# A new instruction order for a group of a two-level Strassen-like matmul, fills in one operation, W as one tile

## The chip, the cores and the metric

The kernel runs on one core of one Trainium2 chip. The metric is the time of one execution in microseconds (us), as the device measures it; lower is better. One run of it was also taken by the hardware profiler, and all lines shown here come from that profiled execution.

## The reference

The reference makes a running sum of `x` along the rows and takes neighbouring differences of it, which gives `x` back but for rounding, and multiplies by `w`:

```python
B, S, D = 8, 2048, 2048
cs = np.cumsum(x, axis=1)
diff = cs - np.concatenate([zeros((B, 1, D)), cs[:, :-1, :]], axis=1)
return np.matmul(diff, w).astype(np.float32)
```

So what has to be computed is `x @ w` with `x` of 16384 x 2048 and `w` of 2048 x 2048, float32 in and out.

## The kernel before

The 16384 rows are 128 row tiles of 128 rows (`t`). The first four are multiplied plainly in bf16 while `w` comes in from HBM; the next four (`group_plain`) and the four after those (`group_half`) go over to the scheme of the main part. The main part is 29 groups of four row tiles each (`class Group`), and these make most of the time.

**Arithmetic of a group.** The four tiles of a group are called g, h, k, l. Two pairs of tiles and the halves of `w` form one level of a seven-product scheme (Winograd's form of Strassen's), and five of its seven products (`P1` to `P5`) are split once more in the same way, into seven quarters `p1` to `p7`. A quarter is four matmuls of 128x512 (`quarter`, line 561); `P6` and `P7` aren't split and are made in eight steps of four matmuls each (`steps`, line 542). That makes 5 x 7 + 2 x 8 = 51 PE steps and 204 matmuls a group. In the step names `P3.p2` is quarter p2 of product P3, and `P6h.1` a step of P6 for tiles of h.

**Around the matmuls.** Every row tile comes as two halves of 512 KB: `load0`, `load1` (line 100, SP queue, into the five slots of the tile `F`), `weigh0`, `weigh1` (ACT, line 112: sum of absolute values), `scale` (two small DVE instructions, lines 128 and 130), `unit` (POOL, line 136), `narrow0`, `narrow1` (ACT, line 147: to fp16, in place), and `turn0`, `turn1` (line 160: DMA transposes on the SP queue into the x tiles). DVE then makes the sums of halves: `S1` to `S4` over whole tiles and `P1.s1` and the like over quarters (line 532). Results come out of PSUM banks by `keep` (ACT, line 569: scale into a buffer `c`), `add` (DVE, line 572: scale and add into the same buffer) and `put` (line 583: 256 KB to HBM on the SP queue). There are seven such buffers in a first-in, first-out list `free`: a `keep` takes the head, a `put` gives its buffer back at the tail. Copies and merges between banks are `P1.cg`, `P1.ct`, `P2.cv` (ACT, line 1014) and `P1.m1`, `P1.m2` (DVE, line 1021). Banks go the same way through the list `open_banks`.

**The passing buffer.** Weights of the second level that have no place of their own pass through one tile `flow` of four blocks of 512: by DVE (`P1.fp4`, `P3.fp2`, `P5.fp4`, `P5.fp5`, line 928, four subtractions or additions of 512 columns each), or from HBM (`P2.fp4`, `P4.fp4`, line 525, 512 KB). A fill has to wait until the quarter that used the buffer before has been read out.

**What sets the order.** It is written out by hand in the string `ORDER`: names of steps with the group that they belong to, as an offset (`load0.g+1` is the load of the next group). Each round of the loop walks the string once, and `after` chains each instruction to the one before it on its engine, so every engine, and the SP queue, runs its instructions in exactly this order. `END_ORDER` is the order of the last steps of the last group. Two pieces of preparation stand in the first group only: `before` puts two subtractions ahead of `P1.s4` and four (`in_5.third`) ahead of `P5.s3`.

Of the kernel before, what the change touches and what calls it, by code (L numbers as in the profile page):

```python
# [10 lines left out]
def kernel(  # L11
# [6 lines left out]
    nc = tc.nc  # L18
    P = 128
# [28 lines left out]


    const = ctx.enter_context(tc.tile_pool(name="const", bufs=1))  # L50
    W = [const.tile([P, 4 * NH], f32, name=f"W{k}") for k in range(KH)]
    whole = [t.rearrange("p (a h n) -> p a h n", a=2, h=2) for t in W]
    pieces = [
        t.bitcast(f16).rearrange("p (i n j c) -> p i j n c", i=4, j=2, c=NB) for t in W
    ]
    B11, T1, B12, T2, B21, T3, B22, T4 = (
        [p[:, i // 2, i % 2] for p in pieces] for i in range(8)
    )
    uw = const.tile([P, 1], f32, name="uw")
    uinv = const.tile([P, 1], f32, name="uinv")  # L60

# [29 lines left out]
    unit = {}  # L91
# [4 lines left out]
    def load(t, i):  # L96
        if t < END:
            after(
                "sp",
                lambda: nc.sync.dma_start(  # L100
                    where[t][i], x2[ds(t * P, P), ds(i * NH, NH)]
                ),
            )
# [51 lines left out]
    def turn(t, halves=range(2)):  # L155
        if t < END:
            for i in halves:
                after(
                    "sp",
                    lambda: nc.sync.dma_start_transpose(  # L160
                        place(t)[i], narrowed(t)[:, ds(i * NH, NH)]
                    ),
                )

    def alone(shape, dtype, name, until=ctx):
        pool = until.enter_context(tc.tile_pool(name=f"{name}_", bufs=1))
        return pool.tile(shape, dtype, name=name)

    with ExitStack() as head:
# [138 lines left out]
        for ko in range(KO - KQ):  # L308
# [9 lines left out]
            if ko in turns:  # L318
                q, a = turns[ko]
# [149 lines left out]
    spills = ctx.enter_context(  # L469
        tc.tile_pool(name="spills", bufs=1, space=bass.MemoryType.DRAM)  # L470
    )
    S1 = [alone([P, 2, NB], f16, f"S1{i}") for i in range(2)]
    inner = alone([P, 20, NB], f16, "inner")
    flow = alone([P, 4, NB], f16, "flow")
    spill = [spills.tile([P, 4, NB], f16, name=f"spill{i}") for i in range(1, 3)]
# [43 lines left out]
    passed = [flow[:, k, :] for k in range(4)]  # L519
# [15 lines left out]
    def steps(to, a, b, first, pieces):  # L535
        for i in range(pieces):
            ks = range(i * KH // pieces, (i + 1) * KH // pieces)

            def some():
                for k in ks:  # L540
                    for n in range(2):
                        said = nc.tensor.matmul(  # L542
                            to[n],
                            a[k],
                            b[k][:, n, :],
                            start=(first and k == 0),
                            stop=(k == KH - 1),
                            skip_group_check=True,
                        )
# [42 lines left out]
    def parts(t):  # L592
        return [Part(a.rearrange("p (n k) m -> p n (k m)", n=2)) for a in place(t)]
# [16 lines left out]
    in_2, in_3 = Inner(B21), Inner(B22)  # L610
    in_3.Q4 = [spare.pop() for _ in range(4)]
    in_4, in_5 = Inner(T4), Inner(T1)
    for i in (in_2, in_4, in_5):
        i.Q4 = passed
    assert not spare
    in_1 = Inner(B11, (in_5.Q1, [t.all[:, n, :] for t in reversed(S1) for n in range(2)]))

    def group_plain(g, X, Y, Z, V):
        h = g + 2
# [122 lines left out]
    def group_half(g, X, Y, q, e, v, w):  # L742
# [179 lines left out]
        put(C21h[0], h + 1, 0)  # L922
        turn(next_l, [1])

    def fill_by(op, a, b):
        def some():
            for k in range(4):
                after("dve", lambda: nc.vector.tensor_tensor(passed[k], a[k], b[k], op))  # L928

        return some  # L930

    sevens = {
        "P1": (in_1, {"p4": fill_by(SUB, in_1.t21, in_1.Q2)}),
        "P2": (in_2, {"p4": lambda: bring_flow(1)}),
        "P3": (in_3, {"p2": fill_by(ADD, in_3.Q4, in_3.Q2)}),
        "P4": (in_4, {"p4": lambda: bring_flow(2)}),
        "P5": (
            in_5,
            {
                "p4": fill_by(SUB, in_5.t21, in_5.Q2),  # L940
                "p5": fill_by(SUB, in_5.t22, in_5.Q2),
            },
        ),
    }
# [3 lines left out]
    class Group:  # L948
# [112 lines left out]
        def plan(self):  # L1061
# [46 lines left out]
            for a, b in ("gk", "hl"):  # L1108
                (A11, A12), (A21, A22) = half[a], half[b]
                self.step(f"S1.{a}", total, A21, A21, A22, ADD)  # L1110
                self.step(f"S2.{a}", total, A11, A21, A11, SUB)
# [73 lines left out]
                    self.step(f"{P}{c}.{j}", some, a, to, j)  # L1185

    ORDER = """
    P2.s3+0 keep.C11g0+0 P1.p2+0 load0.g+1 P1.s3+0 keep.C21h0-1 P1.p3+0 P1.p7+0
    P2.cv+0 S1.g+0 S2.g+0 P2.s4+0 P2.p6+0 P1.m2+0 keep.C11h1+0 add.C21h0.x-1
    load1.g+1 P1.fp4+0 turn0.l+0 P2.p2+0 P5.p1+0 add.C11h1.e+0 add.C11g0.v+0  # L1190
    keep.C11g1+0 P6g.0+0 turn1.l+0 add.C11g1.q+0 S1.h+0 P5.s1+0 put.C12g1-1
    put.C21h0-1 weigh0.g+1 P1.p4+0 S2.h+0 P2.p3+0 add.C11g1.e+0 P5.cg+0 P2.fp4+0
    S4.g+0 P2.p7+0 P5.s2+0 weigh1.g+1 load0.h+1 P5.p2+0 scale.g+1 unit.g+1
    put.C11g0+0 keep.C11h0+0 add.C11h1.q+0 load1.h+1 P6g.2+0 weigh0.h+1 P6h.1+0
    P6g.1+0 P5.s4+0 P2.p4+0 P5.s3+0 P6g.3+0 keep.C22g0+0 P6h.0+0 P5.fp5+0 S4.h+0
    P3.s1+0 narrow0.g+1 P5.p5+0 P5.ct+0 put.C21h1-1 put.C11h1+0 keep.C12g0+0
    load0.k+1 weigh1.h+1 keep.C12g1+0 P4.s1+0 put.C11g1+0 P3.fp2+0 P5.p6+0
    narrow1.g+1 S3.g+0 add.C11h0.q+0 put.C11h0+0 P6h.2+0 put.C21g1-1 scale.h+1
    P6h.3+0 keep.C12h1+0 P3.s2+0 P3.s4+0 P3.p2+0 P3.p1+0 load1.k+1 P7g.1+0
    add.C12g0.q+0 P7g.2+0 keep.C12h0+0 P3.p6+0 narrow0.h+1 P7g.3+0 add.C12g0.z+0  # L1200
    P7g.0+0 S3.h+0 P7h.2+0 P3.s3+0 turn1.g+1 add.C12g1.q+0 P3.p7+0 P5.m1+0
    P5.p7+0 unit.h+1 turn0.g+1 P5.fp4+0 weigh0.k+1 narrow1.h+1 add.C22g0.x+0
    put.C22g0+0 P7h.1+0 weigh1.k+1 P7h.0+0 load1.l+1 unit.l+0 add.C12h1.q+0
    scale.k+1 put.C12g0+0 unit.k+1 narrow0.k+1 narrow1.k+1 P5.p3+0 keep.C22g1+0
    P5.m2+0 keep.C22h1+0 add.C12h0.q+0 load0.l+1 P5.p4+0 add.C12h1.z+0 P4.s3+0
    P4.fp4+0 P7h.3+0 P4.s2+0 P4.s4+0 add.C22h1.x+0 add.C22g1.x+0 put.C22g1+0
    P4.p1+0 P4.p2+0 turn0.h+1 keep.C22h0+0 keep.C21g0+0 P3.p5+0 add.C12g1.e+0
    P3.p3+0 add.C22h0.x+0 turn1.k+1 put.C22h0+0 put.C22h1+0 add.C21g0.x+0
    add.C12h1.e+0 P4.p6+0 P3.p4+0 turn1.h+1 add.C12g1.z+0 add.C12h0.z+0
    put.C12h1+0 P1.s1+1 P4.p5+0 keep.C21g1+0 weigh0.l+1 P1.p1+1 P1.cg+1  # L1210
    put.C21g0+0 P4.p3+0 P4.p4+0 keep.C21h1+0 add.C21g1.x+0 turn0.k+1
    add.C21g1.q+0 put.C12h0+0 P2.p1+1 P4.p7+0 P1.s2+1 P1.p5+1 P1.s4+1 weigh1.l+1
    P1.p6+1 add.C21h1.e+0 P2.s1+1 P1.ct+1 scale.l+1 add.C21h1.q+0 P1.m1+1
    narrow0.l+1 narrow1.l+1 P2.s2+1 P2.p5+1
    """
    ORDER = [(s[:-2], int(s[-2:])) for s in ORDER.split()]
    early = max(n for _, n in ORDER)
# [15 lines left out]
        for s in ("load0", "load1", "weigh0", "weigh1", "scale", "unit", "narrow0", "narrow1", "turn0", "turn1"):  # L1233
            del groups[0].do[f"{s}.{c}"]
    del groups[1].do["load0.g"], groups[1].do["load1.g"]
    before = {"P1.s4": lambda: less(in_1.Q2[2:], in_1.t22[2:], in_1.Q1[2:]), "P5.s3": in_5.third}
    for b in range(-early, len(groups) - late):
        for name, ahead in ORDER:
            i = b + ahead
# [39 lines left out]
```

## Time and profile before

| | |
|---|---|
| median of 3 runs | 1502.03 us (1501.6 to 1503.25) |
| the profiled execution, its own time | 1505.42 us |
| its span, first to last instruction | 1503.6 us |
| mean granted clock of TensorE | 0.996 |
| busy: PE / DVE / ACT / POOL | 1456.9 / 1284.5 / 973.5 / 60.5 us |
| HBM read / written | 181.40 / 135.27 MB |

Busy PE is overlapped time: a 128x512 matmul is shown with about 379 ns from start to end, while the next one starts well before that end. So a short hold of PE does not show as idle time in full. A row of a timeline holds equal instructions that follow each other, with the start, the time from the first start to the last end, their number, and in brackets the idle time before them and what ended it.

### The profile page before, as it was taken

How to read it: one execution, taken by the hardware profiler on the slowest of the kernel's cores; microseconds unless marked ns; L12 is line 12 of the kernel's file. 1: busy time of each engine (PE TensorE's matmuls, PEld its weight loads, DVE VectorE, ACT ScalarE, POOL GpSimd, SP SyncE). 2: the span in 40 equal slices, each digit the busy share in tenths (PEclk: the TensorE clock that was granted, in tenths of full speed). 3: DMA queues.
4: the chain of work that ended last, by engine and by line, in shares of the span. 5: the costliest groups of instructions: out<-in, count | busy, mean ns of one | idle time of the engine just before them, and what ended most of it. 6: DMA issues, size and time to landing. Idle time of an engine off the chain costs nothing.

```text
span 1503.6 us, 20817 instructions
## 1 busy us (share of the span) xinstructions
PE 1456.9 (97%) x6679; PEld 652.7 (43%) x6679; DVE 1284.5 (85%) x2645; ACT 973.5 (65%) x1446; POOL 60.5 (4%) x136
## 2 busy tenths in 40 slices
PE   8999999999999999999999999999999999999998
PEld 3444444444444444444444444444444444444443
DVE  7999988887888888888888788888889888888887
ACT  5887466665666766666657566666676566676662
POOL 0110000000000000000000000000000000000000
PEclk9999999999999999999999999999999999999999
DMA  9999888899899999889999889998899988899984
GB/s 364 360 245 276 235 242 258 258 246 263 217 257 259 253 269 242 234 262 256 252 252 236 245 261 246 273 243 257 249 264 251 275 236 255 252 253 263 259 225 147
DMA packets 386397, 383.09 MB, mean 255 GB/s; under 512 B 275760, under 2 KB 275760, under 8 KB 386160
## 3 DMA queue, kind: packets, MB, share of 16 engines
q1 hardware_dynamic: 385728, 379.93, 90.2%
q0 software_dynamic: 560, 1.84, 0.3%
q8 instruction: 52, 0.85, 0.2%
q14 instruction: 57, 0.47, 0.1%
HBM read 181.40 MB, written 135.27 MB: 211 GB/s over the span
## 4 chain that ended last, share of the span: by engine, by line
PE 67%; DMA 17%; DVE 11%; ACT 3%; issue 2%; SPq 1%; DVEq 0%; ACTq 0%
PE b L561 38%; PE b L542 26%; DMA x<-F 10%; DVE c L572 4%; DMA out_dram<-c 4%; DVE x L532 3%; PE b L264 2%; DVE inner L532 2%; DMA W<-in_w_dram 2%; DMA F<-in_x_dram 1%; ACT c L569 1%; DVE b L1021 1%; ACT F L147 1%; SPq L160 1%; DMA W<-in_x_dram 0%
## 5 line engine op out<-in xcount | busy, mean ns | idle before, releaser
L572 DVE SCALAR_TENSOR_TENSOR c<-b,of,c 128x512 f32<-128x512 f32 x790 | 564.2, 744 | 114.7 <-ACT c L569 70.6
L542 PE MATMUL b<-W,x 128*128 128x512 f16 x2144 | 509.3, 381 | 20.0 <-ACT c L569 15.5
L569 ACT ACTIVATE c<-b,of 128x512 f32<-128x512 f32 x492 | 321.7, 683 | 276.2 <-PE b L561 137.3
L561 PE MATMUL b<-W,x 128*128 128x512 f16 x1892 | 453.0, 379 | 10.9 <-DVE c L572 10.8
L561 PEld LDWEIGHTS <-x 128*128 128x128 f16 x2488 | 243.4, 98 | 318.7 <-issue 33.6
L112 ACT ACTIVATE waste<-F 128x1024 uint8<-128x1024 f32 x246 | 259.0, 1053 | 113.6 <-DMA F<-in_x_dram 113.0
L542 PEld LDWEIGHTS <-x 128*128 128x128 f16 x2144 | 210.4, 98 | 278.9 <-issue 16.2
L147 ACT ACTIVATE F<-F,of 128x1024 f16<-128x1024 f32 x246 | 282.0, 1146 | 53.8 <-DVE of L130 51.5
L532 DVE TENSOR_TENSOR x<-x,x 128x1024 f16<-128x1024 f16 (+1 forms) x388 | 221.4, 583 | 43.9 <-DMA x<-F 37.4
L561 PEld LDWEIGHTS <-inner 128*128 128x128 f16 x1648 | 161.2, 98 | 195.3 <-DVE inner L532 1.7
L561 PE MATMUL b<-W,inner 128*128 128x512 f16 x944 | 232.8, 379 | 0.5 <-DVE inner L532 0.5
L561 PE MATMUL b<-flow,x 128*128 128x512 f16 x588 | 151.7, 380 | 4.1 <-DVE c L572 4.0
L561 PE MATMUL b<-inner 128*128 128x512 f16 x472 | 121.1, 379 | 0.0
L136 POOL TENSOR_SCALAR of<-of,uw 128x1 f32<-128x1 f32 x124 | 55.6, 459 | 1337.2 <-DVE of L128 1329.2
L928 DVE TENSOR_TENSOR flow<-W 128x512 f16<-128x512 f16 x232 | 82.8, 418 | 6.0 <-PE b L561 5.8
L1021 DVE TENSOR_TENSOR b<-b,c 128x512 f32<-128x512 f32 x116 | 80.0, 690 | 2.5 <-PE b L561 2.4
L1014 ACT COPY b<-b 128x512 f32<-128x512 f32 x87 | 50.1, 575 | 24.4 <-PE b L561 13.1
L264 PE MATMUL b<-wb,xP 128*128 128x512 bf16 x240 | 57.4, 393 | 4.5 <-ACT wb L248 3.1
L1014 ACT COPY c<-b 128x512 f32<-128x512 f32 x58 | 33.6, 580 | 37.5 <-PE b L561 37.4
L532 DVE TENSOR_TENSOR inner<-x 128x512 f16<-128x512 f16 x117 | 49.3, 422 | 7.6 <-DMA x<-F 5.2
L532 DVE TENSOR_TENSOR inner<-x,inner 128x512 f16<-128x512 f16 x117 | 49.2, 421 | 4.0
L532 DVE TENSOR_TENSOR inner<-inner,x 128x512 f16<-128x512 f16 x117 | 48.4, 413 | 0.1
(69 smaller groups left out, 528.7 us busy)
## 6 DMA issues: line engine op xcount, KB each, us to landing
F<-in_x_dram SPq DMA_DIRECT2D x246, 512.0 KB, 5.9
out_dram<-c SPq DMA_DIRECT2D x492, 256.0 KB, 3.4
flow<-spill SPq DMA_DIRECT2D x58, 512.0 KB, 4.4
W<-in_w_dram SPq DMA_DIRECT2D x32, 512.0 KB, 9.5
W<-in_x_dram SPq DMA_DIRECT2D x16, 256.0 KB, 7.5
x<-F SPq DMA_TRANSPOSE x246, 3.5
out_dram<-o POOLq DMA_DIRECT2D x5, 256.0 KB, 4.0
out_dram<-o SPq DMA_DIRECT2D x5, 256.0 KB, 3.5
```

The costliest lines, as they stand in the source:

```text
L112: lambda: nc.scalar.activation(waste, where[t][i], ABS, scale=1.0 / ROW, accum_out=sums_of[t][:, i : i + 1],),
L136: after("pool", lambda: nc.gpsimd.tensor_scalar(u, m, uw, None, MUL))
L147: lambda: nc.scalar.activation(narrowed(t)[:, ds(i * NH, NH)], where[t][i], COPY, scale=s),
L264: lambda: nc.tensor.matmul(ps[r][n], xP[:, r, ko, :], wb[h, ko][:, ds(n * NB, NB)], start=(ko == 0), stop=(ko == KO - 1),),
L532: after("dve", lambda: nc.vector.tensor_tensor(dst.all, p.all, q.all, op))
L542: said = nc.tensor.matmul(to[n], a[k], b[k][:, n, :], start=(first and k == 0), stop=(k == KH - 1), skip_group_check=True,)
L561: said = nc.tensor.matmul(to, a[k], b[k], start=(first and k == 0), stop=(k == 3), skip_group_check=True)
L569: after("act", lambda: nc.scalar.activation(c, p, COPY, scale=u))
L572: after("dve", lambda: nc.vector.scalar_tensor_tensor(c, p, u, c, MUL, ADD))
L928: after("dve", lambda: nc.vector.tensor_tensor(passed[k], a[k], b[k], op))
L1014: after("act", lambda: nc.scalar.copy(c, p))
L1021: after("dve", lambda: nc.vector.tensor_tensor(t, p, s, ADD))
```

## The change

There are three parts to it. `W` becomes one tile instead of eight, and `S1` one tile instead of two, so that a view can reach over four blocks (`quarter_of`, `spare_of`). `fill_by` then makes one DVE instruction of 2048 columns instead of four of 512. For this the blocks of `in_1.Q2` lie in `S1` in the opposite order, and the two halves of its preparation change places (one in `group_half`, one in `before`). And the string `ORDER` is another permutation of the same steps; in it some steps belong to another round than before (for example `load0.g+2` in place of `load0.g+1`). `END_ORDER` stays.

```diff
--- before.py
+++ after.py
@@ -48,7 +48,8 @@
 
 
     const = ctx.enter_context(tc.tile_pool(name="const", bufs=1))
-    W = [const.tile([P, 4 * NH], f32, name=f"W{k}") for k in range(KH)]
+    W_all = const.tile([P, KH, 4 * NH], f32, name="W")
+    W = [W_all[:, k, :] for k in range(KH)]
     whole = [t.rearrange("p (a h n) -> p a h n", a=2, h=2) for t in W]
     pieces = [
         t.bitcast(f16).rearrange("p (i n j c) -> p i j n c", i=4, j=2, c=NB) for t in W
@@ -56,6 +57,16 @@
     B11, T1, B12, T2, B21, T3, B22, T4 = (
         [p[:, i // 2, i % 2] for p in pieces] for i in range(8)
     )
+    blocks = W_all.bitcast(f16).rearrange(
+        "p k (i n j c) -> p i j k n c", i=4, j=2, c=NB
+    )
+
+    def quarter_of(i, a, n):
+        return blocks[:, i // 2, i % 2, ds(4 * a, 4), n, :]
+
+    def spare_of(i, k):
+        return blocks[:, i // 2, i % 2, ds(k, 2), :, :]
+
     uw = const.tile([P, 1], f32, name="uw")
     uinv = const.tile([P, 1], f32, name="uinv")
 
@@ -469,7 +480,8 @@
     spills = ctx.enter_context(
         tc.tile_pool(name="spills", bufs=1, space=bass.MemoryType.DRAM)
     )
-    S1 = [alone([P, 2, NB], f16, f"S1{i}") for i in range(2)]
+    S1_all = alone([P, 4, NB], f16, "S1")
+    S1 = [S1_all[:, ds(2 * i, 2), :] for i in range(2)]
     inner = alone([P, 20, NB], f16, "inner")
     flow = alone([P, 4, NB], f16, "flow")
     spill = [spills.tile([P, 4, NB], f16, name=f"spill{i}") for i in range(1, 3)]
@@ -613,7 +625,7 @@
     for i in (in_2, in_4, in_5):
         i.Q4 = passed
     assert not spare
-    in_1 = Inner(B11, (in_5.Q1, [t.all[:, n, :] for t in reversed(S1) for n in range(2)]))
+    in_1 = Inner(B11, (in_5.Q1, [S1_all[:, i, :] for i in range(4)]))
 
     def group_plain(g, X, Y, Z, V):
         h = g + 2
@@ -887,7 +899,7 @@
         unit_of(next_l)
         in_4.third()
         load(then, 1)
-        less(in_1.Q2[:2], in_1.t22[:2], in_1.Q1[:2])
+        less(in_1.Q2[2:], in_1.t22[2:], in_1.Q1[2:])
 
         a11, a12, a22, s1, s2, s3, s4 = A4
         Q = in_4
@@ -922,23 +934,26 @@
         put(C21h[0], h + 1, 0)
         turn(next_l, [1])
 
+    def in_twos(t):
+        return t if len(t.shape) == 4 else t.rearrange("p (a b) n -> p a b n", a=2)
+
     def fill_by(op, a, b):
         def some():
-            for k in range(4):
-                after("dve", lambda: nc.vector.tensor_tensor(passed[k], a[k], b[k], op))
+            x, y = (in_twos(t) for t in (a, b))
+            after("dve", lambda: nc.vector.tensor_tensor(in_twos(flow), x, y, op))
 
         return some
 
     sevens = {
-        "P1": (in_1, {"p4": fill_by(SUB, in_1.t21, in_1.Q2)}),
+        "P1": (in_1, {"p4": fill_by(SUB, quarter_of(0, 1, 0), S1_all)}),
         "P2": (in_2, {"p4": lambda: bring_flow(1)}),
-        "P3": (in_3, {"p2": fill_by(ADD, in_3.Q4, in_3.Q2)}),
+        "P3": (in_3, {"p2": fill_by(ADD, spare_of(2, 0), inner[:, 16:20, :])}),
         "P4": (in_4, {"p4": lambda: bring_flow(2)}),
         "P5": (
             in_5,
             {
-                "p4": fill_by(SUB, in_5.t21, in_5.Q2),
-                "p5": fill_by(SUB, in_5.t22, in_5.Q2),
+                "p4": fill_by(SUB, quarter_of(1, 1, 0), quarter_of(6, 1, 0)),
+                "p5": fill_by(SUB, quarter_of(1, 1, 1), quarter_of(6, 1, 0)),
             },
         ),
     }
@@ -1185,33 +1200,33 @@
                     self.step(f"{P}{c}.{j}", some, a, to, j)
 
     ORDER = """
-    P2.s3+0 keep.C11g0+0 P1.p2+0 load0.g+1 P1.s3+0 keep.C21h0-1 P1.p3+0 P1.p7+0
-    P2.cv+0 S1.g+0 S2.g+0 P2.s4+0 P2.p6+0 P1.m2+0 keep.C11h1+0 add.C21h0.x-1
-    load1.g+1 P1.fp4+0 turn0.l+0 P2.p2+0 P5.p1+0 add.C11h1.e+0 add.C11g0.v+0
-    keep.C11g1+0 P6g.0+0 turn1.l+0 add.C11g1.q+0 S1.h+0 P5.s1+0 put.C12g1-1
-    put.C21h0-1 weigh0.g+1 P1.p4+0 S2.h+0 P2.p3+0 add.C11g1.e+0 P5.cg+0 P2.fp4+0
-    S4.g+0 P2.p7+0 P5.s2+0 weigh1.g+1 load0.h+1 P5.p2+0 scale.g+1 unit.g+1
-    put.C11g0+0 keep.C11h0+0 add.C11h1.q+0 load1.h+1 P6g.2+0 weigh0.h+1 P6h.1+0
-    P6g.1+0 P5.s4+0 P2.p4+0 P5.s3+0 P6g.3+0 keep.C22g0+0 P6h.0+0 P5.fp5+0 S4.h+0
-    P3.s1+0 narrow0.g+1 P5.p5+0 P5.ct+0 put.C21h1-1 put.C11h1+0 keep.C12g0+0
-    load0.k+1 weigh1.h+1 keep.C12g1+0 P4.s1+0 put.C11g1+0 P3.fp2+0 P5.p6+0
-    narrow1.g+1 S3.g+0 add.C11h0.q+0 put.C11h0+0 P6h.2+0 put.C21g1-1 scale.h+1
-    P6h.3+0 keep.C12h1+0 P3.s2+0 P3.s4+0 P3.p2+0 P3.p1+0 load1.k+1 P7g.1+0
-    add.C12g0.q+0 P7g.2+0 keep.C12h0+0 P3.p6+0 narrow0.h+1 P7g.3+0 add.C12g0.z+0
-    P7g.0+0 S3.h+0 P7h.2+0 P3.s3+0 turn1.g+1 add.C12g1.q+0 P3.p7+0 P5.m1+0
-    P5.p7+0 unit.h+1 turn0.g+1 P5.fp4+0 weigh0.k+1 narrow1.h+1 add.C22g0.x+0
-    put.C22g0+0 P7h.1+0 weigh1.k+1 P7h.0+0 load1.l+1 unit.l+0 add.C12h1.q+0
-    scale.k+1 put.C12g0+0 unit.k+1 narrow0.k+1 narrow1.k+1 P5.p3+0 keep.C22g1+0
-    P5.m2+0 keep.C22h1+0 add.C12h0.q+0 load0.l+1 P5.p4+0 add.C12h1.z+0 P4.s3+0
-    P4.fp4+0 P7h.3+0 P4.s2+0 P4.s4+0 add.C22h1.x+0 add.C22g1.x+0 put.C22g1+0
-    P4.p1+0 P4.p2+0 turn0.h+1 keep.C22h0+0 keep.C21g0+0 P3.p5+0 add.C12g1.e+0
-    P3.p3+0 add.C22h0.x+0 turn1.k+1 put.C22h0+0 put.C22h1+0 add.C21g0.x+0
-    add.C12h1.e+0 P4.p6+0 P3.p4+0 turn1.h+1 add.C12g1.z+0 add.C12h0.z+0
-    put.C12h1+0 P1.s1+1 P4.p5+0 keep.C21g1+0 weigh0.l+1 P1.p1+1 P1.cg+1
-    put.C21g0+0 P4.p3+0 P4.p4+0 keep.C21h1+0 add.C21g1.x+0 turn0.k+1
-    add.C21g1.q+0 put.C12h0+0 P2.p1+1 P4.p7+0 P1.s2+1 P1.p5+1 P1.s4+1 weigh1.l+1
-    P1.p6+1 add.C21h1.e+0 P2.s1+1 P1.ct+1 scale.l+1 add.C21h1.q+0 P1.m1+1
-    narrow0.l+1 narrow1.l+1 P2.s2+1 P2.p5+1
+    keep.C11g1+0 add.C11h1.e+0 P2.p2+0 add.C11g1.q+0 add.C21g1.x-1 P2.p3+0
+    turn1.l+0 add.C11g1.e+0 P6g.3+0 P2.s3+0 P5.p1+0 P5.cg+0 P2.fp4+0 P6g.1+0
+    weigh0.g+1 S1.h+0 P5.s1+0 keep.C11h0+0 P5.s2+0 P2.p7+0 add.C11h1.q+0
+    put.C21g0-1 load1.g+1 S2.h+0 P6g.0+0 put.C21h1-1 P6g.2+0 add.C11g0.v+0
+    keep.C12g1+0 P5.s4+0 P2.p4+0 put.C11h1+0 add.C11h0.q+0 P5.p6+0 P5.fp5+0
+    P6h.1+0 put.C21g1-1 load0.h+1 S4.g+0 weigh1.g+1 P6h.0+0 keep.C12g0+0
+    put.C11h0+0 P5.p2+0 keep.C22g0+0 put.C11g1+0 S3.g+0 P5.p5+0 S4.h+0 P6h.2+0
+    P5.ct+0 P3.s1+0 P7g.2+0 P5.m1+0 scale.g+1 narrow0.g+1 P6h.3+0 P5.s3+0
+    P4.s1+0 P5.p7+0 put.C11g0+0 P7g.0+0 P5.fp4+0 P5.m2+0 load1.h+1 P7g.3+0
+    P4.s2+0 S3.h+0 narrow1.g+1 P5.p4+0 load0.k+1 load1.k+1 keep.C12h0+0 P7g.1+0
+    keep.C12h1+0 P3.fp2+0 P3.s2+0 turn0.g+1 P5.p3+0 weigh0.h+1 add.C22g0.x+0
+    put.C22g0+0 P3.s4+0 P4.s4+0 P3.p2+0 weigh1.h+1 P7h.0+0 keep.C22g1+0
+    add.C12g0.z+0 keep.C22h0+0 add.C22g1.x+0 scale.h+1 P4.fp4+0 P3.s3+0 P7h.2+0
+    put.C22g1+0 P3.p1+0 add.C12g0.q+0 turn1.g+1 narrow0.h+1 keep.C22h1+0
+    add.C12h1.z+0 P7h.1+0 P7h.3+0 add.C22h0.x+0 add.C22h1.x+0 put.C22h0+0
+    P3.p6+0 add.C12g1.q+0 P3.p3+0 weigh0.k+1 P3.p5+0 P3.p4+0 add.C12g1.z+0
+    P4.s3+0 weigh1.k+1 narrow1.h+1 keep.C21h1+0 add.C12h0.z+0 add.C12g1.e+0
+    scale.k+1 add.C12h1.e+0 unit.k+1 P3.p7+0 P4.p1+0 keep.C21g0+0 P4.p2+0
+    P4.p5+0 put.C12g0+0 P4.p6+0 turn0.h+1 narrow0.k+1 P1.p1+1 add.C12h1.q+0
+    P4.p4+0 add.C21g0.x+0 keep.C21g1+0 P1.s1+1 P1.s2+1 P1.p5+1 put.C22h1+0
+    P1.s3+1 P1.cg+1 unit.h+1 narrow1.k+1 P1.ct+1 add.C21g1.q+0 P1.s4+1 load0.l+1
+    weigh0.l+1 add.C12h0.q+0 load1.l+1 put.C12g1+0 add.C21h1.e+0 P1.p6+1 P1.m1+1
+    P1.fp4+1 weigh1.l+1 scale.l+1 narrow0.l+1 P4.p3+0 P4.p7+0 add.C21h1.q+0
+    keep.C21h0+0 turn1.h+1 P2.s1+1 P1.p3+1 narrow1.l+1 turn0.k+1 P1.p7+1
+    unit.g+1 P1.p2+1 P2.p1+1 put.C12h1+0 keep.C11g0+1 turn1.k+1 put.C12h0+0
+    P1.m2+1 P1.p4+1 P2.s2+1 P2.s4+1 add.C21h0.x+0 P2.cv+1 load0.g+2 keep.C11h1+1
+    S1.g+1 S2.g+1 P2.p5+1 unit.l+1 turn0.l+1 put.C21h0+0 P2.p6+1
     """
     ORDER = [(s[:-2], int(s[-2:])) for s in ORDER.split()]
     early = max(n for _, n in ORDER)
@@ -1233,7 +1248,7 @@
         for s in ("load0", "load1", "weigh0", "weigh1", "scale", "unit", "narrow0", "narrow1", "turn0", "turn1"):
             del groups[0].do[f"{s}.{c}"]
     del groups[1].do["load0.g"], groups[1].do["load1.g"]
-    before = {"P1.s4": lambda: less(in_1.Q2[2:], in_1.t22[2:], in_1.Q1[2:]), "P5.s3": in_5.third}
+    before = {"P1.s4": lambda: less(in_1.Q2[:2], in_1.t22[:2], in_1.Q1[:2]), "P5.s3": in_5.third}
     for b in range(-early, len(groups) - late):
         for name, ahead in ORDER:
             i = b + ahead
```

## The prediction

> **What bounds the kernel now.** I read the page first, then stretches of the span, PE's timeline, the waits, the chain that ended last, and SP's and DVE's timelines.
>
> ```profile
> span 1503.6 us, 20817 instructions
> q1 hardware_dynamic: 385728, 379.93, 90.2%
> ```
> ```profile
> 541.70:586.70 45.00, 44.52 (x205) 19.92 (x204) 39.12 (x83) 29.82 (x46) 1.60 (x4) 1.00 0.92 258
> 818.30:867.10 48.80, 45.93 (x205) 20.36 (x204) 39.01 (x83) 29.92 (x46) 1.59 (x4) 0.97 0.89 239
> 1184.50:1228.70 44.20, 44.20 (x205) 19.94 (x204) 39.05 (x83) 29.80 (x46) 1.60 (x4) 1.00 0.90 261
> 175.90:1456.90 1281.00, 1248.82 (x5714) 559.59 (x5713) 1092.53 (x2300) 831.84 (x1257) 44.53 (x112) 1.00 0.91 252
> ```
> ```profile
> 1219.09 4.48 PE L561 MATMUL b<-W,x 128*128 128x512 f16 x20
> 1224.27 2.02 PE L561 MATMUL b<-W,x 128*128 128x512 f16 x8
> 1489.76 1.89 PE L561 MATMUL b<-W,x 128*128 128x512 f16 x8
> 1493.10 4.48 PE L561 MATMUL b<-W,x 128*128 128x512 f16 x20 [1.45 <-DVE c L572]
> ```
>
> The four rows of stretches give PE, weight loads, DVE, ACT and POOL busy, then granted clock, DMA share and GB/s. The first three are one group each and hold the same work; they took 45.0, 48.8 and 44.2 us. Matmuls follow each other every (4.48 - 1.89) / 12 = 0.216 us, so a group's 204 need 44.06 us and a PE step of four 0.864. The 44.2 row is a group in which PE hardly waited. DVE is busy for 39 us of it, ACT for 30, and the transfers, by their share, for 40 to 43. Everything fits under PE, with little room. The long stretch holds 28 groups: 5714 x 0.216 = 1234.2 us of matmuls in 1281.0. **So 46.8 us, 1.67 a group, are lost to waits**, and the last wait (1.45, and 0.16 covered by the matmul before it) adds 1.6. That is all that an order can win; the head (175.9 us) and the matmuls stay.
>
> ```profile
> ACT waste L112 <- DMA F<-in_x_dram: 113.0, 45, 5.1
> ACT c L569 <- DMA out_dram<-c: 100.0, 98, 4.0
> DVE x L532 <- DMA x<-F: 37.4, 28, 3.2
> PE b L542 <- ACT c L569: 15.5, 13, 2.9
> PE b L561 <- DVE c L572: 14.9, 30, 1.5
> ```
> ```profile
> 817.56 6.57 DMA F<-in_x_dram
> ...
> 824.15 0.95 ACT waste L112
> ...
> 825.36 5.46 DMA out_dram<-c
> ...
> 830.91 0.70 ACT c L569
> ...
> 831.64 3.56 PE b L542 x8
> ```
> ```profile
> 817.56 0.89 SPq L100 DMA_DIRECT2D F<-in_x_dram  x2
> 818.55 6.75 SPq L160 DMA_TRANSPOSE x<-F  x2
> 825.36 2.16 SPq L583 DMA_DIRECT2D out_dram<-c  x2
> ```
>
> The waits (us in total, times, longest) show two kinds on PE: 15.5 us behind a `keep`, 14.9 behind an `add`. The chain and SP's timeline of the same place, in the 48.8 us group, show how the first arises. Two loads and two transposes go onto SP one behind the other and hold it until 825.3; only then is the store of a finished buffer issued (`put.C12g1` of the group before). It lands at 830.8, `keep.C11h0` gets its buffer, and `P6h.1`, which overwrites the bank that this reads, starts at 831.64. The clock falls behind such a wait (0.97 in this row, two more groups like it): 45.93 - 44.3 = 1.6 us each, 5 in all.
>
> **The change part by part.** *W as one tile* moves no instruction and, by the order of both programs, leaves the head's waits as they were but for one sum that waits for two stores more; I cost it at nothing (if that sum, far ahead of its use, is late: under 1 us, once).
>
> *Fills.*
>
> ```profile
> 1199.92 1.42 DVE L928 TENSOR_TENSOR flow<-W,inner 128x512 f16<-128x512 f16 x4
> 1201.26 0.68 DVE L532 TENSOR_TENSOR x<-x,x 128x1024 f16<-128x1024 f16 x1
> 1201.86 0.74 DVE L572 SCALAR_TENSOR_TENSOR c<-b,of,c 128x512 f32<-128x512 f32 x1
> ```
> ```profile
> 729.00 0.69 DVE L1021 TENSOR_TENSOR b<-b,c 128x512 f32<-128x512 f32 x1
> 729.60 0.74 DVE L572 SCALAR_TENSOR_TENSOR c<-b,of,c 128x512 f32<-128x512 f32 x1
> ```
> ```profile
> L928 DVE TENSOR_TENSOR flow<-W 128x512 f16<-128x512 f16 x232 | 82.8, 418 | 6.0 <-PE b L561 5.8
> L1021 DVE TENSOR_TENSOR b<-b,c 128x512 f32<-128x512 f32 x116 | 80.0, 690 | 2.5 <-PE b L561 2.4
> L446 DVE TENSOR_TENSOR W<-W 128x1024 f16<-128x1024 f16 x8 | 4.9, 682 | 0.0
> L1014 ACT COPY c<-b 128x512 f32<-128x512 f32 x58 | 33.6, 580 | 37.5 <-PE b L561 37.4
> ```
>
> Four of 512 columns occupy DVE for 1201.26 - 1199.92 = 1.34 us; 512 more columns cost 0.68 - 0.42 = 0.265. One fill of 2048 is then 0.42 + 3 x 0.265 = 1.22 us long and holds DVE for 1.13: 0.21 saved, four times a group, 0.84 of 39 us. DVE isn't the bound, so this is worth nothing by itself. Against it, PE's first matmul of the quarter used to wait for 0.42 us of the fill and now waits for 1.22. The tightest place is `P3.fp2`: between `P5.p4`, which reads the buffer last, and `P3.p2` the new list has two PE steps, 1.73 us, less 0.16 for the last matmul's end: 1.57. 1.22 and two signals of 0.05 fit, with 0.25 to spare.
>
> A rule speaks against it. The Trainium skill, "VectorE: DVE Perf Modes", section "What auto-detection actually checks", gives two 16-bit inputs the double pace only at steps of one, and the new inputs jump between blocks; its tier table has 2293 ns for 2048 columns at the single pace. Line 446's row has such jumps (two rows of 512) and takes 682 ns, like the contiguous 0.68, so I take the double pace; a single-pace bound from line 1021's 690 ns is 0.69 + 3 x 0.53 = 2.3 us, a rival below.
>
> *The order.* I laid both orders over a PE that never waits: PE steps at 0.864 us, every other instruction behind its engine's previous one and its inputs, with the durations shown. A DMA is counted behind those in front of it on the one queue. The old order then has eight transfers that land just when somebody already waits for them (`turn1.l`, `load0.h`, `put.C11h0`, `put.C12g0`, `put.C22h0`, `turn0.h`, `turn1.h`, `turn0.g`), and `put.C12g1` 0.15 us ahead. In the new order none does: the closest are `turn1.l` for `S1.h` (0.8), `put.C22g0` for `keep.C22h1` (0.9) and `load1.g` for its `weigh` (1.5). Following the seven buffers, `keep.C11h0` now takes the one of the previous `put.C21h0`, 4.6 us after it lands; `put.C12g1` stands early behind two loads, 4.7 us ahead of need. The wait at `P6h.1` goes, its clock loss too. What is late next there is `S2.h`, 1.8 us early.
>
> On DVE the old order had three places without margin (`P4.p7`, `P2.p4`, `P5.p1`); the 2.02 row above against 1.89 is `P4.p7` losing 0.13, at a margin that I count as zero. In the new one the closest is `P2.p5`, whose bank `add.C21h0.x` frees: from `P1.p7`'s end there are three PE steps, 2.59 - 0.16 = 2.43 us; `P1.m2` (0.59), `P2.s2` and `P2.s4` (0.34 each), the add (0.74) and three signals make 2.2, 0.1 to 0.2 to spare. Then `P3.p2` (0.25) and `P5.p7` (0.36). A margin of 0.1 can be lost: bounds 0 and, if the four closest each lose 0.13, 0.5 a group. I take one loss of 0.13, nearest to the row seen: 28 x 0.13 = 3.6 us. In the first group `P5.s3` has four subtractions ahead, 1.34 - 0.36 = 1.0 late, once. At the end `P4.p5` no longer waits 1.6 for adds (the C12 adds stand earlier); 0.1 is left at `P4.p6`.
>
> **Sum**: 46.8 - 3.6 - 1.0 + 1.5 = 43.7 us less. The profiled execution took 1505.42 us, span and 1.8 around it, 3.4 over the median; counted as a fixed offset, the median falls from 1502.0 to 1458. Own range: 1453 (nothing lost) to 1470 (0.5 a group).
>
> **The rivals.**
>
> ```profile
> F<-in_x_dram SPq DMA_DIRECT2D x246, 512.0 KB, 5.9
> out_dram<-c SPq DMA_DIRECT2D x492, 256.0 KB, 3.4
> x<-F SPq DMA_TRANSPOSE x246, 3.5
> ```
> ```profile
> L160 SPq DMA_TRANSPOSE x<-F x246: 1231/1292/5082, 64.5 to 1458.5; - x123
> L583 SPq DMA_DIRECT2D out_dram<-c x492: 332/432/1566, 87.9 to 1500.2; - x164
> ```
> ```profile
> L569 ACT ACTIVATE c<-b,of 128x512 f32<-128x512 f32 x492 | 321.7, 683 | 276.2 <-PE b L561 137.3 <-DMA out_dram<-c 100.0 <-DVE b L1021 21.3
> L112 ACT ACTIVATE waste<-F 128x1024 uint8<-128x1024 f32 x246 | 259.0, 1053 | 113.6 <-DMA F<-in_x_dram 113.0
> L112 ACT ACTIVATION_READ_ACCUMULATOR waste<-F 128x1 f32 x246 | 47.2, 192 | 0.0
> ```
>
> *1. Only the buffer wait goes*, because DVE's margins of a few tenths don't hold: 15.5 + 13 x 0.16 + 5 = 22.6 us won, 1479. For it: 14.9 us in 30 waits behind adds now. Against: those are the places that I count at zero. Chance 0.09.
>
> *2. Slower: a ring through four landings.* In the new order one chain comes back to its start a group later: `turn1.l`, `S1.h`, `put.C11h1`, `keep.C22g0`, `P5.m1`, `P3.fp2`, `put.C22g0`, `keep.C22h1`, `add.C22h0.x`, `load0.l`, `weigh`, `scale.l`, `add.C21h0.x`, and SP again. Between its landings lie some 21.8 us of instructions (DVE: nine of 0.34, two of 0.60, two fills of 1.13, six adds of 0.74, three merges of 0.59, which is how far apart the rows at 729 start, and two scales; ACT: two keeps of 0.68, a copy of 0.58 and two weighings of 1.05 + 0.19; SP: the issue of four stores at 0.43 and of a transpose at 1.29; signals). With the medians above (3.5, 3.4, 3.4, 5.9) the ring takes 38.0, and PE's 44.06 decides; from landings of 24.0 in sum, 7.8 over the medians, a group takes today's 45.75. Transfers closer together could do that: 379.93 MB in 90.2% of the span is 0.28 MB/us, so a group's 11.5 MB take 41 of 44.06 us. At 2.1 us late each: 46.4 a group, 1502 + 28 x 0.65 = 1520. Against: the 44.2 us group had all transfers in it at a share of 0.90. Chance 0.04.
>
> *3. The landings grow, but less.* "DMA: Bandwidth & Descriptors" of the Trainium skill, section "Latency and other measured facts", has 0.2 us on average for HBM's latency and 2 at high load. No run here shows that spread. A ring with 1.8 us more at each landing, by my count of rows, takes 45.2: 28 x 0.55 = 15 us won, 1487. Chance 0.04.
>
> *4. The fill runs at the single pace*, 1.07 longer: `P3.p2` 0.82 late, `P1.p4` 0.4, perhaps `P5.p4` 0.3, so 1.2 to 1.5 of the 1.67 us come back: 1496, at the upper end no change. Chance 0.05, of which 0.02 within 0.2%.
>
> **How the numbers follow.** Forecast 0.78, rivals 0.09, 0.04, 0.04, 0.05. The range 1453 to 1481 holds the forecast and rival 1. A measurement of this kernel tells 0.2% (3 us) from no change: faster 0.78 + 0.09 + 0.04 + 0.03 = 0.94, same 0.02, slower 0.04.
>
> **What the profile after would show.** Right: stretches of a group near 44.2 us with a clock of 1.00; no wait of PE behind line 569's successor; waits of ACT for stores and loads mostly gone; a fill of about 1220 ns, 116 of them; DVE busy for some 38 us a group. Wrong: fills of 2300 ns (rival 4); PE waiting behind adds in many groups (1); landings 2 us over the medians, with SP held behind transposes and every group long (2, 3).

## The result: 1478.78 us, little over half of the gain that was forecast

| | before | after |
|---|---|---|
| median on one chip | 1502.64 us (1501.6 to 1503.52, 4 runs) | 1478.78 us (1475.78 to 1480.64, 4 runs) |
| the profiled execution, its own time | 1505.42 us | 1478.89 us |
| its span | 1503.6 us | 1477.1 us |

The ratio is 0.984, 95% interval 0.9822 to 0.9858: 23.9 us won, where 44 were forecast (1458).

The page of the changed kernel, its span and the queue that SP feeds, and the issues (operation, number, KB, median us to landing):

```profile
span 1477.1 us, 20442 instructions
q1 hardware_dynamic: 385728, 379.93, 95.7%
F<-in_x_dram SPq DMA_DIRECT2D x246, 512.0 KB, 6.1
out_dram<-c SPq DMA_DIRECT2D x492, 256.0 KB, 4.4
x<-F SPq DMA_TRANSPOSE x246, 4.8
```

Three stretches: a group without a wait, one with, and the 28 groups:

```profile
631.00:675.00 44.00, 44.00 (x206) 19.93 (x205) 38.50 (x70) 29.40 (x44) 1.08 (x4) 1.00 0.99 258
675.00:720.90 45.90, 44.40 (x205) 19.93 (x204) 38.52 (x70) 30.46 (x45) 1.07 (x4) 1.00 0.98 253
182.90:1436.30 1253.40, 1237.44 (x5714) 558.59 (x5712) 1080.87 (x1964) 848.97 (x1261) 30.15 (x112) 1.00 0.98 257
```

The floor of 44.06 us a group is reached (44.00), and no clock loss is left, but the 28 groups take 1253.4 and not the forecast 1238 or so. The waits (us in total, times, longest) say at which kind of place:

```profile
PE b L573 <- DVE c L584: 16.0, 22, 1.3
DVE c L584 <- ACT c L581: 43.5, 57, 1.9
ACT c L581 <- DMA out_dram<-c: 41.5, 38, 2.4
```

The wait of PE behind a `keep` (15.5 before) is gone. PE now waits behind an `add`, the `add` behind a `keep`, and the `keep` behind a store that has not landed. Which steps these are follows from the order of the program: each matmul that starts more than 0.216 us after the one before it was put down to its step and the excess summed, matmuls at the slow clock apart, for every kernel below.

| lost in the main part, us | sum | `P6h.1` | `P2.p4` | `P4.p7` | `P5.p1` | `P2.p3` | `P2.p5` | `P1.p4` |
|---|---|---|---|---|---|---|---|---|
| before | 50.9 | 22.8 | 7.0 | 6.8 | 6.2 | | | |
| after | 23.7 | | 1.9 | | | 14.9 | 2.2 | 0.3 |

The four places of before are gone or small now (the rest of the 50.9 was the slow clock, `P4.p5` and the start; of the 23.7, the start and `P5.p7`). In their stead `P2.p3` is late in 17 groups, by up to 1.43. One of them, the sum that starts at 723.20, on SP, ACT, DVE and PE (start, length, what, idle time before and its end; the stores there are still those of the group before):

```profile
706.37 0.89 SPq L111 DMA_DIRECT2D F<-in_x_dram  x2
707.35 0.40 SPq L595 DMA_DIRECT2D out_dram<-c  x1
707.80 6.80 SPq L171 DMA_TRANSPOSE x<-F  x2
714.69 0.53 SPq L595 DMA_DIRECT2D out_dram<-c  x1
715.31 1.29 SPq L171 DMA_TRANSPOSE x<-F  x1
716.69 0.53 SPq L595 DMA_DIRECT2D out_dram<-c  x1
```
```profile
714.11 1.06 ACT L123 ACTIVATE waste<-F 128x1024 uint8<-128x1024 f32 x1 [0.20 <-DMA F<-in_x_dram]
...
721.62 1.27 ACT L581 ACTIVATE c<-b,of 128x512 f32<-128x512 f32 x2 [1.83 <-DMA out_dram<-c]
```
```profile
722.39 1.41 DVE L584 SCALAR_TENSOR_TENSOR c<-b,of,c 128x512 f32<-128x512 f32 x2 [1.81 <-ACT c L581]
```
```profile
723.20 1.02 PE L573 MATMUL b<-W,inner 128*128 128x512 f16 x4 [1.27 <-DVE c L584]
```

SP issues `load0.l` and `load1.l`, `put.C12g1`, and then two transposes, `turn1.h` and `turn0.k`, whose issue takes 6.80 us in place of the 2.6 that two of 1.29 make. So `put.C12h1` leaves at 714.69 and `put.C12h0`, one transpose later, at 716.69. `keep.C11h1` wants the buffer of the latter and starts at 721.62, the add that frees the bank at 722.39, `P2.p3` at 723.20. It is the pattern of the old wait (a store behind two transposes behind two loads) at another place of the list.

### The profile page after: what moved, and what is told of

It reads as the page before. It is cut to its first block, busy times and chain, and to the rows that moved or that the text cites. A ratio compares the mean times of both kernels' runs of the same rounds, so it can differ in the third digit from the quotient of the medians.

```text
span 1477.1 us, 20442 instructions
## 1 busy us (share of the span) xinstructions
PE 1443.7 (98%) x6679; PEld 651.2 (44%) x6679; DVE 1272.8 (86%) x2297; ACT 987.7 (67%) x1446; POOL 44.6 (3%) x136
## 3 DMA queue, kind: packets, MB, share of 16 engines
q1 hardware_dynamic: 385728, 379.93, 95.7%
## 4 chain that ended last, share of the span: by engine, by line
PE 79%; DMA 13%; DVE 4%; ACT 3%; issue 1%; SPq 0%; DVEq 0%; ACTq 0%
PE b L573 46%; PE b L554 31%; DMA out_dram<-c 5%; DMA x<-F 4%; DVE c L584 2%; PE b L275 2%; DMA W<-in_w_dram 2%; DMA F<-in_x_dram 2%; ACT waste L123 1%; ACT c L581 1%; DMA W<-in_x_dram 0%; DVE inner L544 0%; ACT c L1029 0%; ACT wb L259 0%; DVE x L544 0%
## 5 line engine op out<-in xcount | busy, mean ns | idle before, releaser
L573 PE MATMUL b<-W,inner 128*128 128x512 f16 x944 | 237.5, 379 | 14.4 <-DVE c L584 12.2
L573 PE MATMUL b<-inner 128*128 128x512 f16 x472 | 116.4, 379 | 1.3 <-DVE c L584 1.2
L147 POOL TENSOR_SCALAR of<-of,uw 128x1 f32<-128x1 f32 x124 | 39.7, 334 | 1327.6 <-DVE of L139 1319.8
L943 DVE TENSOR_TENSOR flow<-W 128x2048 f16<-128x2048 f16 x58 | 70.5, 1216 | 0.0
L943 DVE TENSOR_TENSOR flow<-W,inner 128x2048 f16<-128x2048 f16 x29 | 35.5, 1225 | 27.1 <-PE b L573 27.1
```

The costliest lines, as they stand in the source:

```text
L147: after("pool", lambda: nc.gpsimd.tensor_scalar(u, m, uw, None, MUL))
L573: said = nc.tensor.matmul(to, a[k], b[k], start=(first and k == 0), stop=(k == 3), skip_group_check=True)
L943: after("dve", lambda: nc.vector.tensor_tensor(in_twos(flow), x, y, op))
```

## The experiments

A ratio is against runs of the kernel before on the same chip. The first four kernels below stand against 1507.73 us; the moved store, the two with `turn1.h` and the first with old fills against 1508.97; the other three against 1505.12.

**The fills alone.** New fills and `W` as one tile, old `ORDER`:

```diff
- for k in range(4):
-     after("dve", lambda: nc.vector.tensor_tensor(passed[k], a[k], b[k], op))
+ x, y = (in_twos(t) for t in (a, b))
+ after("dve", lambda: nc.vector.tensor_tensor(in_twos(flow), x, y, op))
  ...
```

> One-operation fills and W and S1 as one tile, with the old order. If the gain of the change is the order's, this stays within 3 us of the kernel before: about 1500 us, since the 0.8 us of DVE time saved per group lie on an engine with 5 us to spare, and the wait of P6h.1 behind the store buffer stays. If the fills had a share in the gain, because the old order has places without any margin on DVE, it would be 1490 or less.

1512.48 us, ratio 1.0029 (1.0014 to 1.0044): no gain, a hair slower. `P6h.1` lost 32.5 us of 59.0 in its profile. Why the old wait was longer with shorter fills is open.

**The order alone.** New `ORDER`, with the two lines marked - above for a fill, and `W` as eight tiles.

> The new order with the old fills of four operations and W in eight tiles. If the order makes the gain, about 1482 us: the changed kernel's 1479 and some 3 us because DVE has 0.8 us more to do per group and the closest margins (P2.p5, 0.1 us) are lost by a part of it. If the one-operation fills are what lets the new order run, 1490 or more.

1479.58 us, ratio 0.9816 (0.9793 to 0.984). The order makes the whole gain, and `P2.p3` loses 13.3 us here as well: it isn't the fills' doing.

**The stores ahead of the turns of k.**

```diff
- turn0.k+1 P1.p7+1 unit.g+1 P1.p2+1 P2.p1+1 put.C12h1+0 keep.C11g0+1 turn1.k+1 put.C12h0+0
+ P1.p7+1 unit.g+1 P1.p2+1 P2.p1+1 put.C12h1+0 keep.C11g0+1 put.C12h0+0 turn0.k+1 turn1.k+1
```

> The changed kernel with the two transposes turn0.k and turn1.k moved on the SP queue to behind the stores put.C12h1 and put.C12h0. Theory A: P2.p3 is late because turn1.h and turn0.k, behind the loads load0.l and load1.l, hold SP, so that put.C12h0 leaves some 4 us late and keep.C11h1 waits for its buffer; then this takes back most of the 14.9 us lost at P2.p3: about 1465 us, unless turn1.k now lands too late for S1.g, which would show as DVE waiting for a transpose. Theory B: P2.p3 is late because DVE itself is behind; then no gain, 1479 or more, since the transposes come later.

1465.81 us, ratio 0.9722 (0.9699 to 0.9746): theory A, 13 us under the changed kernel and 13.8 under the order alone, which ran on the same chip. Its SP and ACT at the same place, and a group:

```profile
704.89 2.97 SPq L171 DMA_TRANSPOSE x<-F  x1
707.96 1.99 SPq L595 DMA_DIRECT2D out_dram<-c  x2
710.05 4.67 SPq L171 DMA_TRANSPOSE x<-F  x2
```
```profile
716.70 1.26 ACT L581 ACTIVATE c<-b,of 128x512 f32<-128x512 f32 x2
```
```profile
1248.30:1292.40 44.10, 44.10 (x206) 19.99 (x205) 39.01 (x71) 30.23 (x46) 1.08 (x4) 1.00 1.00 261
```

The turns still hold SP (4.67 for two), but the two stores no longer stand behind them, `keep.C11h1` finds its buffer, and `P2.p3` loses 3.5 us in place of 14.9. Transfers are as busy as ever (a share of 1.00 in a group of 44.1 us), so it was not their amount.

**The two stores off SP.** `put.C12h1` and `put.C12h0` issued from POOL:

```diff
+ def put_by_pool(c, t, at):
+     after("pool", lambda: nc.gpsimd.dma_start(out2[ds(t * P, P), ds(at * NB, NB)], c))
+     free.append(c)
  ...
- self.step(f"put.{c}", lambda: put(self.at.pop(c), self.row(c), n))
+ go = put_by_pool if c in POOLED else put
+ self.step(f"put.{c}", lambda: go(self.at.pop(c), self.row(c), n))
```

> The changed kernel with the stores put.C12h1 and put.C12h0 issued from POOL's queue, so that SP's transposes cannot hold them. Theory A (SP is held, the buffer comes late): the wait at P2.p3 goes, about 1463 us. Theory B (DVE is behind): no change, 1479. Theory C (the transfers themselves are too slow, the DMA share being 95.7%): the stores land as late as before although they leave earlier, no change, 1479.

1520.12 us, ratio 1.0084 (1.0063 to 1.0104). None of the three theories gave this. The issues, SP, the chain and PE of one place:

```profile
out_dram<-c SPq DMA_DIRECT2D x434, 256.0 KB, 4.5
out_dram<-c POOLq DMA_DIRECT2D x58, 256.0 KB, 8.5
```
```profile
260.18 10.40 SPq L171 DMA_TRANSPOSE x<-F  x3
```
```profile
260.18 11.44 DMA x<-F
```
```profile
272.74 1.46 PE L573 MATMUL b<-flow,x 128*128 128x512 f16 x4 [2.33 <-DVE b L1041]
```

Without the stores between them three transposes follow each other on SP and hold it for 10.40 us; the first lands after 11.44, DVE's merges wait behind the sum that needs it, and `P1.p4` loses 29.7 us of 64.5. The stores from POOL take 8.5 us to land where SP's take 4.5, and `P2.p3` still loses 10.2 us: this run changed the transposes and the landing of the stores at once, and doesn't tell what either is worth.

**Before, with one store moved.** This is the prediction's reading of the old wait, by itself.

```diff
- P1.p2+0 load0.g+1 ... load1.g+1 ... turn0.l+0 ... turn1.l+0 ... put.C12g1-1
+ P1.p2+0 put.C12g1-1 load0.g+1 ... load1.g+1 ... turn0.l+0 ... turn1.l+0
```

> The kernel before with one step moved in its list: the store put.C12g1 of the group before goes from behind load0.g, load1.g, turn0.l and turn1.l to ahead of load0.g, on the same SP queue; nothing else is touched. Theory A (the store is late because SP is held by the transposes behind the loads, and this alone makes the wait at P6h.1): the waits at P6h.1 (22 to 34 us in the profiles of the old order) go, the four other places (P2.p4, P4.p7, P5.p1, P4.p5, some 22 us) stay, so 20 to 30 us less than before: a ratio of 0.980 to 0.987. Theory B (with so many transfers under way some other landing is as late there, turn1.l or turn0.l for S1.h and S2.h, now 0.4 us later still): the wait changes its place and the time stays within 0.3% of before.

1516.33 us, ratio 1.0061 (1.0035 to 1.0087): theory B. SP, ACT, DVE and PE in one group:

```profile
591.59 6.05 SPq L160 DMA_TRANSPOSE x<-F  x2
```
```profile
599.27 0.68 ACT L569 ACTIVATE c<-b,of 128x512 f32<-128x512 f32 x1
```
```profile
601.19 0.69 DVE L532 TENSOR_TENSOR x<-x,x 128x1024 f16<-128x1024 f16 x1 [2.89 <-DMA x<-F]
```
```profile
603.01 1.90 PE L542 MATMUL b<-W,x 128*128 128x512 f16 x8 [1.63 <-DVE x L532]
```

The store is on time now and `keep.C11h0` runs without a wait, but `S1.h` waits 2.89 us for `turn1.l`, and `P6h.1`, which also needs what DVE makes from it, is as late as before (21.4 us in all). Two landings were late side by side, both held by the same two loads. `P2.p4` grew to 20.7, as its add stands behind `S1.h` on DVE.

**Before, with the store and the two turns moved**, and the weighing that would then wait for the loads put back (the places that the moved steps left are not shown):

```diff
- P1.p2+0 load0.g+1
+ P1.p2+0 put.C12g1-1 turn0.l+0 turn1.l+0 load0.g+1
- keep.C11h0+0 add.C11h1.q+0
+ keep.C11h0+0 weigh0.g+1 weigh1.g+1 add.C11h1.q+0
- P5.s3+0 P6g.3+0
+ P5.s3+0 scale.g+1 unit.g+1 P6g.3+0
```

> The kernel before with the store and the two late turns moved: put.C12g1 of the group before, turn0.l and turn1.l go ahead of load0.g on SP; and, so that nothing on ACT and DVE waits for the loads that this puts back, weigh0.g and weigh1.g go behind keep.C11h0, scale.g and unit.g behind P5.s3. With the store alone moved, S1.h waited for turn1.l and P6h.1 lost as much as before. Theory A (at P6h.1 two landings were late side by side, the store's and the transpose's, both because SP is held behind the load pair; both have to start earlier): P6h.1 loses under 5 us in place of 21 to 23, P2.p4 does not grow, and the run is 15 to 28 us under before, a ratio of 0.981 to 0.990. Theory B (in the old order any transfer that is put back, here the loads of g and what stands behind them, makes the next wait): another place loses what P6h.1 wins, within 0.5% of before or slower.

1474.84 us, ratio 0.98 (0.9782 to 0.9819): theory A, a little beyond its numbers (30 us), and seven moved steps of the old list give at least as much as the whole new one. SP at this place, PE's first wait, a group:

```profile
624.51 2.67 SPq L160 DMA_TRANSPOSE x<-F  x2
627.23 1.07 SPq L100 DMA_DIRECT2D F<-in_x_dram  x2
```
```profile
PE b L561 <- DVE c L572: 9.9, 16, 1.5
```
```profile
580.20:624.40 44.20, 44.20 (x206) 20.00 (x205) 38.96 (x84) 29.78 (x46) 1.60 (x4) 1.00 0.91 261
```

The same two transposes, now ahead of the loads, take 2.67 us in place of 6.05. `P6h.1` loses nothing, `P2.p4` 1.7; `P4.p7` (6.9) and `P5.p1` (6.4) stay, as they have other causes.

**After, with `turn1.h` ahead of the loads**, and that together with the turns of k behind the stores.

```diff
- P1.s4+1 load0.l+1 weigh0.l+1 ... load1.l+1 put.C12g1+0 ... keep.C21h0+0 turn1.h+1
+ P1.s4+1 turn1.h+1 load0.l+1 weigh0.l+1 ... load1.l+1 put.C12g1+0 ... keep.C21h0+0
```

> The changed kernel with one step moved: turn1.h goes from behind load0.l, load1.l and put.C12g1 to ahead of load0.l; both late turns of k stay ahead of put.C12h1 and put.C12h0. Theory A (a transpose holds SP only when it stands close behind loads or another transpose; turn1.h and turn0.k hold it for 3.3 us each): turn1.h holds SP for about 1.3 us now, the stores leave some 2 to 4 us earlier, P2.p3 loses 0 to 4 us in place of 14.9, and the time is 1465 to 1471. Theory B (the hold is that of the transfers in flight, wherever the transpose stands): turn0.k takes the hold over, P2.p3 loses 10 us or more, 1475 to 1480.

> The changed kernel with both moves: turn0.k and turn1.k behind put.C12h0, and turn1.h ahead of load0.l. Theory A (only the hold of SP ahead of the two stores costs time): most of the 3.5 us that P2.p3 still lost with the turns of k moved goes as well, 1461 to 1465. Theory B (what is left there comes from the length of landings alone): no change against the kernel with the turns of k moved, 1465 to 1468, or longer if turn1.h in its new place stands back to back with turn0.h.

1475.41 us (ratio 0.9775, 0.976 to 0.9789) and 1477.83 (0.9792, 0.9775 to 0.9808). SP, DVE and PE of the first:

```profile
704.32 1.39 SPq L171 DMA_TRANSPOSE x<-F  x1
706.12 0.93 SPq L111 DMA_DIRECT2D F<-in_x_dram  x2
707.12 0.42 SPq L595 DMA_DIRECT2D out_dram<-c  x1
707.66 1.58 SPq L171 DMA_TRANSPOSE x<-F  x1
...
710.22 3.00 SPq L171 DMA_TRANSPOSE x<-F  x1
```
```profile
713.76 0.21 DVE L139 TENSOR_SCALAR of<-of 128x1 f32<-128x1 f32 x1 [1.01 <-ACT waste L123]
...
716.47 0.74 DVE L584 SCALAR_TENSOR_TENSOR c<-b,of,c 128x512 f32<-128x512 f32 x1
```
```profile
717.26 1.02 PE L573 MATMUL b<-inner 128*128 128x512 f16 x4 [0.42 <-DVE c L584]
```

On the hold theory A is right as far as it goes: `turn1.h` takes 1.39 us, `turn0.k` 1.58, and `P2.p3` loses 2.0. The hold is not gone, though: it now falls on `turn1.k` (3.00 here, 2.94 in the median, 1.29 in the changed kernel), with only `put.C12h0` behind it. On the time the theory isn't right: the loads of l now start behind a transpose, `scale.l` waits 1.01 us on DVE for their weighing, and seven instructions later `add.C21h0.x` frees the bank of `P2.p5` late (9.6 us in all, 20 groups). With both moves nothing is left at `P2.p3`, but `P2.p5` loses 11.2 and `P1.p4` 8.7, and the time is longer than either theory's numbers. The load at the head of this DVE chain has no room to give.

**The fills once more, in the order with the turns of k behind the stores:** first the old fills, then both side by side on one chip.

> The new order with turn0.k and turn1.k moved behind put.C12h0, but the fills of the kernel before (four instructions of 512 columns) and W as eight tiles. Theory A (DVE isn't the bound, so a fill in one operation is worth nothing even when the store's wait is gone): the time of the same order with the new fills, 1465.8 within 3 us. Theory B (in the new order DVE stands close enough to the end at P2.p5 and P2.p3 that 0.84 us of DVE a group show once the store is on time): P2.p5 and P2.p3 lose 0.2 to 0.5 us a group more, 1471 to 1480.

> The changed kernel with turn0.k and turn1.k behind put.C12h0, as run before with 1465.8, now beside the same order with the old fills on one chip. Theory A (a fill in one operation is worth nothing in this order): the two agree within 0.15%. Theory B (the shorter hold of DVE shows once the store is on time): this one is 1 to 4 us faster. Theory C (the longer wait for a fill of 1.22 us in place of 0.42 costs): this one is 1 to 4 us slower; the first looks, 1465.8 and 1463.7 against different runs of before, point this way.

> The same order (turn0.k and turn1.k behind put.C12h0) with the four fills of 512 columns and W as eight tiles, run before with 1463.7. Theory A: within 0.15% of the new fills. Theory B: 1 to 4 us slower. Theory C: 1 to 4 us faster.

1463.74 us (ratio 0.97, 0.9686 to 0.9715); then 1465.71 (0.9744, 0.9727 to 0.9761) with the new fills and 1463.82 (0.9732, 0.9716 to 0.9749) with the old. The difference, 1.9 us or 0.13%, lies within theory A and at the lower end of theory C, and the old fills were the lower both times. So the new fills win nothing here; that they cost a little isn't excluded. This order is the fastest found, 13 to 15 us under the changed kernel. Its profiles lose 9.0 to 11.7 us, some 4 of them at the start of the loop.

## Why the prediction came out as it did

**Right.** Group floor and clock: 44.00 us and 1.00; DVE is busy for 38.5 us in a group, where 38 were forecast. One fill:

```profile
L943 DVE TENSOR_TENSOR flow<-W 128x2048 f16<-128x2048 f16 x58 | 70.5, 1216 | 0.0
```

1216 ns against 1.22 us forecast, so the single pace of rival 4 did not come. The prediction read the "step ±1" of the Trainium skill, "VectorE: DVE Perf Modes", section "What auto-detection actually checks", as ruling out inputs that jump between blocks. The section doesn't say that. The same page of the Trainium skill has 2293 ns for the single pace in its table; the trace shows 1216 with such jumps. That the fills are worth nothing by themselves was measured twice. `P4.p6` at the end was 0.08 late (0.1 forecast), `P5.p7` in the first group 0.96 (1.0). DVE's thin margins cost 2.2 at `P2.p5`, 0.35 at `P5.p7` and 0.3 at `P1.p4`, for which 3.6 were charged. The 22.6 us of the old buffer wait went, clock loss included.

**Half right: the cause of that wait.** The chain of waits showed the store, which ended last by the profile; the transpose for `S1.h` was as late beside it, and moving the store alone won nothing. The new order begins the turns of l earlier too: `turn1.l` starts 10.5 us ahead of `P6h.1` in the median, against 8.9 before. That this is what wins here is argued from the kernel with the store and the two turns moved; it wasn't tried in the new order itself.

**Wrong: the margins of the landings in the new order.** The step "in the new order none does" land just when it is needed, with 0.8 as the closest, rests on the issue of a transpose at 1.29 us, the median. Over the 28 of each in the changed kernel's list the median issue is 2.14 for `turn1.h` and 3.65 for `turn0.k`. The row quoted for before had the warning in it (a maximum of 5.08, and 6.75 for two of them at the very place of the old wait); its median hides that the long ones are always the same step (`turn1.l`: 4.48 in the median, no other step of the list over 2.2). With 6.80 us for `turn1.h` and `turn0.k` behind the loads of l in place of 2.6, `put.C12h0` leaves 4.2 us later, and its margin, which the prediction doesn't give, is gone. That is 14.9 us at `P2.p3`, of which 3.5 are left with the turns of k behind the stores. The rest of the gap: 1.9 at `P2.p4`, and the start of the loop lost some 4.0 where 1.0 was charged, as PE also waits once for a sum (`P1.p5`) and once for a merge (`P1.p3`):

```profile
173.76 1.04 PE L573 MATMUL b<-W,inner 128*128 128x512 f16 x4 [1.41 <-DVE inner L544]
...
176.88 1.46 PE L573 MATMUL b<-W,inner 128*128 128x512 f16 x6 [0.86 <-DVE b L1036]
```

The order alone, with `W` as eight tiles, has both of these waits at the same size, so they are the order's. 14.9 + 1.9 + 3.0, less the 0.8 that DVE's margins cost less than charged, is 19.0; with 4.7 charged this makes the 23.7 measured.

**The rivals.** Rival 1 gave 1479, the time that came, by another mechanism: the buffer wait did not simply go while DVE's margins failed, it went to another store, and 14.9 of the 23.7 us stand there. Its sign did show (PE waited for adds 22 times, 16.0 us), so the sign did not tell the two apart. The forecast's own range, 1453 to 1470, missed the time. The wider one, to 1481, holds it only because rival 1's 1479 had been taken in, and as rival 1's mechanism is not what happened, that is luck. Rivals 2 and 3: landings did grow (stores from 3.4 to 4.4 us, transposes from 3.5 to 4.8, loads from 5.9 to 6.1), 19.7 over the ring's four against 16.2, still under the 22.3 (44.06 - 21.8) from which the ring would decide by the prediction's count (its 24.0 is where a group takes the old 45.75); and the order with the turns of k moved has the same landings in groups of 44.1. What the moved `turn1.h` shows is that the tail of that ring (`load`, `weigh`, `scale.l`, `add.C21h0.x`) is the next thing to be late.

## What to carry to other kernels

Price a step on a shared queue at its own place, not at the median of its line: here one transpose took 1.3 or 4.5 us of SP, depending on what stood ahead of it and had not landed yet, and every store behind it waited. When a chain of waits names one late transfer, look for others held by the same thing: only moving all of them won anything. And after a reorder ask first which buffer's store now stands behind the slow issues.

## What the runs showed of the hardware that was not expected

Two DMA transposes behind two loads hold the issuing queue for 6.0 to 6.8 us, ahead of them for 2.67. When the second of the two is let go can be read from the landing times in the traces: its issue ends just before the DMA that stands in front of the first one lands. In the changed kernel `turn0.k` ends 0.11 to 0.23 us before the landing of `put.C12g1` in all 28 groups (in the group shown at 714.60 and 714.74), while the second load landed 0.4 to 0.8 us earlier; in the kernel before, `turn1.l` ends 0.07 to 0.26 us before the landing of `load1.g` in 27 of 28. Loads aren't needed for it: with both moves, where `put.C12h0` stands in front of `turn0.k` and `turn1.k`, the second ends within 0.25 us of that store's landing in all 28, after an issue of 2.72 us in the median. With three in a row (the stores off SP) the match is looser, up to 1.9 us. Why the queue does this, and why the first of two is sometimes long as well (`turn1.h`, 2.14), is open.

The Trainium skill, "DMA: Bandwidth & Descriptors", section "Issuing engines are not separate DMA queues", calls the time to initiate a DMA "usually small relative to the DMA itself". For the store `put.C12h0` shown it is (0.53 us, with the `keep` waiting until 721.62); for these two transposes it is 3.4 us each, as long as a whole landing in the median of before (3.5).

The same 379.93 MB take 90% of the queue's engines in the old order, also at 1474.84 us (0.91 in the group shown), and 95.7% in the new one, where stores and transposes land 1.0 and 1.3 us later and groups without a wait stand at 0.99 and 1.00. So a share near 1 says here how the transfers lie on each other, not that they bound the kernel.
